# One hybrid decoder layer on one core: the stationary forms of the gate products are made earlier and kept in DRAM, and the order of the product stage changes

## The chip, the cores and the metric

The kernel runs on one core of one Trainium2 chip. The metric is the time of one execution in device microseconds (us). TensorE (PE in the profile) multiplies matrices, VectorE (DVE) and ScalarE (ACT) work on elements, GpSimd (POOL) does small arithmetic and issues transfers, SyncE (SP) issues transfers only. Each engine runs its own instructions strictly in order.

## The reference

One layer on a 256 x 2048 activation x, all in float32:

```python
h = rmsnorm(x, pre_norm_g)
proj = h @ w_in        # split: q_a, c_kv, k_rope, z_mla, c_in, b_gate, c_gate, z_conv, g_mla, g_conv
q, k, v = heads of rmsnorm(q_a) @ w_q_b and rmsnorm(c_kv) @ w_kv_b, with rope
attn = causal_softmax(q, k, v) * silu(z_mla)
y_mla = attn @ w_o_mla
u = c_gate * c_in
conv = sum(conv_w[k] * shifted(u, k) for k in range(3))
y_conv = (b_gate * conv * silu(z_conv)) @ w_o_conv
merged = sigmoid(g_mla) * y_mla + sigmoid(g_conv) * y_conv
out = x + rmsnorm(merged @ w_out, post_norm_g)
```

There are 16 heads; every square weight is 2048 x 2048. All weights are read once from DRAM.

## The kernel before, in words

**Split operands.** A float32 product is made of three reduced-precision products. Each operand is split into `hi` (a rounded copy, made by ACT) and `lo` (the rest, made by DVE as operand minus `hi`); the product is hi·hi + hi·lo + lo·hi. `split_act` does the two instructions. A *unit* is 128 x 2048 numbers (1 MB) of weight: SP loads it into one of three `raw` buffers, ACT and DVE split it in two halves of 1024 columns into `whi` and `wlo` (five buffers each), and PE runs 24 matmuls on it. A weight half in one of the five buffers is free again when PE has used it.

**Stages.** First the two latent projections (`qa`, `ckv`), then a loop over 16 heads. Head h runs four weight units of the convolution branch (`channels`, tile `cv`), at every fourth head four units of `z_mla` (`gates`, tile `z`) and, between them, the small products of the attention. At head 0 the latent vectors are also normalised, turned and split. After the heads comes the product stage, on which most of the change lies: a list `seq` of units, each [load, split, matmuls, after], built by hand.

**The product stage.** It makes, per column block c of 512 columns, the gates (`g_mla` = weight 0, `g_conv` = weight 1 of `wsq`), the branch products with `w_o_mla` (weight 2, left operand `at_both`) and `w_o_conv` (weight 3, left operand `cv_both`), and at the end `w_out` (weight 4, left operand `m_both`).
- A *plain* unit (`plain`, `block`) is the 24 matmuls above, on tile `sq`. `gate_block`, `branch_block`, `merged_block` are blocks of four plain units.
- For c = 1, 2, 3 the two gates are made together by seven products of half size instead of eight (`paired`, Strassen's scheme on 2 x 2 blocks of tokens and features). The left operands are seven *forms*, fixed sums of quarters of the normalised x: `11`, `5`, `6`, `7`, `22`, `3`, `12`. The right operands are sums of weight quarters `b`, made by DVE (128 x 2048 additions): products Q1 and Q2 take a loaded quarter as it is, V5, V6, V4 take a sum, V7 takes a sum of its own, V3 a loaded quarter. Each product is two units of 12 matmuls (tiles `sX`, `sY`, `sZ`); each is split by ACT and DVE like a plain unit (`shi`, `slo`, in the same five buffers).
- `make_forms` makes the seven forms at the start of this stage, from x loaded again (`xf`): 16 scalings, four sums `fs`, seven splits into `form`.
- `interleave` says which plain units stand between the products. The loop at the end of the stage issues loads up to four loads ahead and splits two units ahead.
- `turned_unit` brings a branch's left operand back from DRAM, where it was laid down transposed (`far_at`, `far_cv`, `far_m`), into a `raw` buffer and splits it.
- Gates and partial results that are needed later go to DRAM (`keep`) and come back (`again`), all on POOL's queue. `merged_block` fetches its gate and its partial sum in `last`, after its last matmul; then it multiplies, adds, transposes and stores to `far_m`, from where `m_both` is made for the output projection (`out_order`, `out_product`), which follows at once.

SP's queue holds all weight loads in program order; POOL's holds attention's transfers, the taps, `keep`, `again` and `far_m`. ACT's holds two loads near the end.

## Time and profile before

| | |
|---|---|
| median of 3 runs | 1078.97 us (1078.91 to 1081.7) |
| the profiled execution | 1078.8 us, of which the span is 1076.8 us |
| PE busy | 1024.1 us (95%) |
| DVE busy | 802.2 us (74%) |
| ACT busy | 579.4 us (54%) |
| POOL busy | 196.9 us (18%) |
| moved by DMA | 252.14 MB, mean 234 GB/s |

A busy PE is a PE with a matmul in flight; how fast these run is seen from the granted clock (PEclk, a share of full speed) and from the number of matmuls in a stretch. PE has the largest share, so the time is the sum of its matmuls at full speed and of what it loses by waiting and by a lowered clock.

### The profile page before, as it was taken

The numbers are of one execution on the slowest core, as the hardware profiler recorded it, in microseconds if no ns is written. First come the engines' busy times: TensorE is split into PE (matmuls) and PEld (weight loads), VectorE is DVE, ScalarE is ACT, GpSimd is POOL, SyncE is SP. The second block draws the span as 40 slices with busy tenths as digits, with TensorE's granted clock in tenths as the row PEclk, the third lists the DMA queues.
The fourth block names the chain that finished last, engine by engine and source line by source line (L and its number), as shares of the span: only waits on it lengthen the run. The fifth ranks groups of instructions, "written<-read, shape, count | busy, mean of one in ns | idle before, by whom it ended". The sixth has DMA issues, their size and how long they took to land.

```text
span 1076.8 us, 12835 instructions
## 1 busy us (share of the span) xinstructions
PE 1024.1 (95%) x4576; PEld 846.1 (79%) x4576; DVE 802.2 (74%) x1069; ACT 579.4 (54%) x804; POOL 196.9 (18%) x364
## 2 busy tenths in 40 slices
PE   9999999999999999999999976998999899985997
PEld 7888888888888888888888854886887688873786
DVE  7588777787777877768777799879879887644562
ACT  7666545555455564555645474654565555422451
POOL 4610321223212232122231200000001012223000
PEclk9999999999999999999999998998999899997999
DMA  9775875757657577575867973792586455775752
GB/s 366 284 236 200 284 229 207 251 211 261 231 200 253 211 258 237 194 245 207 273 208 268 339 291 142 260 363 86 192 333 233 155 195 211 234 283 208 260 192 79
DMA packets 49824, 252.14 MB, mean 234 GB/s; under 512 B 8768, under 2 KB 11456, under 8 KB 26592
## 3 DMA queue, kind: packets, MB, share of 16 engines
q1 hardware_dynamic: 33984, 205.96, 53.2%
q0 software_dynamic: 15344, 42.07, 11.7%
q10 hardware_dynamic: 432, 3.29, 0.8%
q8 instruction: 36, 0.59, 0.2%
q14 instruction: 28, 0.23, 0.1%
HBM read 226.15 MB, written 20.97 MB: 229 GB/s over the span
## 4 chain that ended last, share of the span: by engine, by line
PE 85%; DVE 7%; DMA 4%; issue 3%; ACT 1%; POOL 1%; ACTq 0%; DVEq 0%; SPq 0%; POOLq 0%
PE cv L88 32%; PE sq L88 16%; PE z L88 8%; PE out L88 6%; PE sX L88 5%; PE sZ L88 2%; PE kn L88 2%; PE qa L88 2%; PE qn L88 2%; PE vv L88 2%; PE ckv L88 2%; PE sY L88 2%; DVE b L1152 1%; DVE wlo L253 1%; PE qr L88 1%
## 5 line engine op out<-in xcount | busy, mean ns | idle before, releaser
L252 ACT ACTIVATE whi<-raw 128x1024 fp32r<-128x1024 f32 (+1 forms) x318 | 324.2, 1031 | 274.5 <-PE cv L88 126.5
L253 DVE TENSOR_TENSOR wlo<-raw,whi 128x1024 fp32r<-128x1024 f32 (+1 forms) x316 | 371.4, 1190 | 128.2 <-ACT whi L252 119.6
L88 PE MATMUL cv<-whi,x_both 128*128 128x512 f32 x1024 | 319.7, 389 | 0.0
L88 PEld LDWEIGHTS cv<-whi,x_both 128*128 128x128 f32 x1024 | 192.3, 188 | 39.5
L88 PE MATMUL cv<-wlo,x_both 128*128 128x512 f32 x512 | 199.5, 390 | 0.0
L88 PEld LDWEIGHTS cv<-wlo,x_both 128*128 128x128 f32 x512 | 96.2, 188 | 19.4
L252 ACT ACTIVATE shi_V<-b 128x1024 fp32r<-128x1024 f32 x60 | 62.3, 1056 | 75.4 <-DVE b L1152 37.1
L253 DVE TENSOR_TENSOR slo_V<-b,shi_V 128x1024 fp32r<-128x1024 f32 x60 | 72.4, 1222 | 24.7 <-ACT shi_V L252 23.4
L88 PE MATMUL sq<-whi,at_both 128*128 128x512 f32 x256 | 80.8, 389 | 0.0
L88 PE MATMUL z<-whi,x_both 128*128 128x512 f32 x256 | 80.0, 389 | 0.0
L88 PE MATMUL sq<-whi,cv_both 128*128 128x512 f32 x256 | 79.8, 389 | 0.0
L88 PE MATMUL out<-whi,m_both 128*128 128x512 f32 x208 | 67.6, 403 | 7.4 <-ACT whi L252 7.4
L336 POOL DMA_DIRECT2D far<-via x64 | 35.3, 558 | 190.5 <-DVE via L328 189.1
L88 PEld LDWEIGHTS sq<-whi,cv_both 128*128 128x128 f32 x256 | 48.1, 188 | 10.0
L88 PEld LDWEIGHTS sq<-whi,at_both 128*128 128x128 f32 x256 | 48.1, 188 | 9.9
L88 PEld LDWEIGHTS z<-whi,x_both 128*128 128x128 f32 x256 | 48.1, 188 | 9.9
L1152 DVE TENSOR_TENSOR b<-b,b 128x2048 f32<-128x2048 f32 x24 | 54.3, 2284 | 0.6 <-DMA b<-wsq_dram 0.6
L88 PEld LDWEIGHTS out<-whi,m_both 128*128 128x128 f32 x208 | 40.7, 196 | 17.1 <-ACT whi L252 8.6
L88 PE MATMUL sq<-wlo,at_both 128*128 128x512 f32 x128 | 49.9, 390 | 3.3 <-DVE wlo L253 3.3
L88 PE MATMUL out<-wlo,m_both 128*128 128x512 f32 x104 | 42.4, 407 | 10.2 <-DVE wlo L253 10.2
L88 PE MATMUL sq<-wlo,cv_both 128*128 128x512 f32 x128 | 49.8, 389 | 0.0
L88 PE MATMUL z<-wlo,x_both 128*128 128x512 f32 x128 | 49.8, 389 | 0.0
(287 smaller groups left out, 1583.5 us busy)
## 6 DMA issues: line engine op xcount, KB each, us to landing
raw<-wcv_dram SPq DMA_DIRECT2D x64, 1024.0 KB, 5.4
raw<-wsq_dram SPq DMA_DIRECT2D x56, 1024.0 KB, 5.3
b<-wsq_dram SPq DMA_DIRECT2D x24, 1024.0 KB, 5.7
raw<-wz_dram SPq DMA_DIRECT2D x16, 1024.0 KB, 4.8
raw<-wqk_dram SPq DMA_DIRECT2D x8, 1024.0 KB, 6.9
cw<-cwr_dram POOLq DMA_DIRECT2D x24, 256.0 KB, 6.2
raw<-wc_dram SPq DMA_DIRECT2D x4, 1024.0 KB, 9.5
raw<-wv_dram SPq DMA_DIRECT2D x4, 1024.0 KB, 5.3
```

The lines of the kernel that those rows point to most:

```text
L88: return tc.keep_in_program_order(nc.tensor.matmul(*a, **kw))
L252: a = nc.scalar.activation(hi, src, AF.Copy)
L253: b = nc.vector.tensor_tensor(lo, src, hi.bitcast(F32), op=ALU.subtract)
L336: tc.keep_in_program_order(queue.dma_start(out=f[i], in_=m))
L1152: nc.vector.tensor_tensor(t[:, :], t[:, :], raw[plus][:, :], op=ALU.add)
```

## The change

1. **Forms among the heads.** `make_forms` becomes a generator that works on half of the features at a time. During heads 1 to 7 it is stepped three times a head. It loads x into an unused part of `at_f` (four 0.5 MB loads on SP's queue), scales, sums into an unused part of `cv_f`, splits into a small pool, and POOL's queue stores each half form to DRAM (`far_form`, 14 stores of 0.5 MB). At the start of the product stage POOL's queue loads the seven forms (1 MB each) into the place where they were made before.
2. **Order of the product stage.** After each of the seven products of a column block stands, in most places, one plain unit; the second gate block of c = 0 is spread over the products of c = 1.
3. **One sum by DMA.** V7's right operand is no longer added by DVE: after V5 has used quarter `(1, k)`, POOL's queue issues an accumulating load of weight quarter `(1, 2 + k)` onto it. Quarter `(1, 2 + k)` is still loaded for V6.
4. **Gate stores on ACT's queue.** `keep` issues on ACT's queue unless the key is a branch product ("m").
5. **Earlier fetches.** `merged_block` fetches the gate and the partial sum after its second unit (one of the two token halves for c = 0 and 1, both for c = 2 and 3, in a pool `late` of their own). The transposed first two blocks come back a block earlier.

```diff
+    def make_forms():
+
+        kq = KH // 2
+        for c in range(2):
+            area = at_f[:, 8:, :].rearrange("p (i k) s -> p i k s", i=2)
+            for i in range(2):
+                nc.sync.dma_start(out=area[:, i], in_=xf[i][:, c * kq * S : (c + 1) * kq * S].rearrange("p (k s) -> p k s", k=kq))
+            yield
+            for i in range(2):
+                for k in range(kq):
+                    x = area[:, i, k, :]
+                    nc.vector.scalar_tensor_tensor(
+                        x, x, col("pre_g", KH * i + kq * c + k), r_x[:, :], op0=ALU.mult, op1=ALU.mult
+                    )
+                yield
...
+            def part(n, src, sign=1.0):
+                f = early_pool.tile([P, kq, 2, P], F32R, name=f"form{n}_{c}", tag="form", bufs=2)
+                hi, lo = f[:, :, 0, :], f[:, :, 1, :]
+                nc.scalar.activation(hi, src, AF.Copy, scale=sign)
+                if sign == 1.0:
+                    nc.vector.tensor_tensor(lo, src, hi.bitcast(F32), op=ALU.subtract)
...
+                return lambda: tc.keep_in_program_order(
+                    nc.gpsimd.dma_start(
+                        out=far_form[n][:, c * w : (c + 1) * w], in_=f[:, :, :, :].rearrange("p k j c -> p (k j c)")
+                    )
+                )
...
+                if s:
+                    tt(*s)
+                go = part(n, src, sign)
+                yield
+                go()
...
+        if 0 < h < 8:
+            next(form_steps)
         channels(h, 2)
+        if 0 < h < 8:
+            next(form_steps)
+        if 0 < h < 8:
+            next(form_steps)
...
+    for n in FORMS:
+        nc.gpsimd.dma_start(out=form[n][:, :, :, :].rearrange("p k j c -> p (k j c)"), in_=far_form[n][:, :])
...
     def keep(key, t):
-        tc.keep_in_program_order(nc.gpsimd.dma_start(out=kept[key][:, :], in_=t[:, :]))
+        queue = nc.gpsimd if key[0] == "m" else nc.scalar
+        tc.keep_in_program_order(queue.dma_start(out=kept[key][:, :], in_=t[:, :]))
...
     def merged_block(c, both):
...
+        def soon():
+            for t in range(1 if c < 2 else NT):
+                fetch(t)
+
         def last(pss):
             for t in range(NT):
...
+                if len(got) <= t:
+                    fetch(t)
+                g, m = got[t]
...
-        return block(c, 3, lambda k: both[k // 4][:, k % 4, :], {}, last)
+        return block(c, 3, lambda k: both[k // 4][:, k % 4, :], {1: soon}, last)
...
                 t = raw[src]
-                if plus:
+                if plus and name[:2] != "V7":
                     nc.vector.tensor_tensor(t[:, :], t[:, :], raw[plus][:, :], op=ALU.add)
+                if name[:2] == "V5":
+                    k = plus[1]
+                    tc.keep_in_program_order(
+                        nc.gpsimd.dma_start(out=raw[1, k][:, :], in_=wsq[1, c, 2 + k], accum_op=ALU.add)
+                    )
...
-    def interleave(s, p, extra):
-        seq.extend(s["Q1"])
-        seq.extend(extra[:1])
-        seq.extend(s["V5"])
-        seq.extend(extra[1:])
-        for name, n in (("", 1), ("V6", 1), ("V7", 1), ("V4", 2), ("V3", 1), ("Q2", 2)):
-            seq.extend(s.get(name, []))
-            seq.extend(p[:n])
-            del p[:n]
+    def interleave(s, after):
+        for name in ("Q1", "V5", "V6", "V7", "V4", "V3", "Q2"):
+            seq.extend(s[name])
+            seq.extend(after.get(name, []))
...
+    interleave(s1, {
+        "Q1": g0[:1], "V5": g0[1:2], "V6": g0[2:3], "V7": g0[3:] + at_u[:1], "V4": at_u[1:] + p[0][:2],
+        "V3": p[0][2:], "Q2": p[1][:3],
+    })
+    interleave(s2, {
+        "Q1": p[1][3:], "V5": p[2][:1], "V6": p[2][1:2], "V7": p[2][2:3], "V4": p[2][3:], "Q2": p[3][:1],
+    })
+    interleave(s3, {
+        "Q1": p[3][1:2], "V5": p[3][2:3], "V6": p[3][3:] + cv_u[:1], "V7": cv_u[1:] + v[0][:1], "V4": v[0][1:3],
+        "V3": v[0][3:], "Q2": v[1],
+    })
```

How the change moves instructions, at three places. A scheduler places what the program does not pin, so the place of an instruction on its engine is not the place of its line.

**DVE at head 0, where the latent vectors are split and the first weight units of the heads follow** (`wlo` rows are weight splits, `z` the first gate product, `at_f` its area and that of x). Before:

```order
L515 SCALAR_TENSOR_TENSOR ckv<-at_f,pv,ckv 128x256 x4
L740 SCALAR_TENSOR_TENSOR at_f<-z_0_637,r_both,at_f 128x512
L328 STREAM_TRANSPOSE cw<-at_f 128x4x4x32
L740 SCALAR_TENSOR_TENSOR at_f<-z_1_638,r_both,at_f 128x512
L253 TENSOR_TENSOR wlo_0_812<-raw_761,whi_0_811 128x512
L253 TENSOR_TENSOR wlo_0_816<-raw_807,whi_0_815 128x1024
L328 STREAM_TRANSPOSE cw<-at_f 128x4x4x32
L253 TENSOR_TENSOR wlo_1024_820<-raw_807,whi_1024_819 128x1024
```

After:

```order
L517 SCALAR_TENSOR_TENSOR ckv<-at_f,pv,ckv 128x256 x4
L840 SCALAR_TENSOR_TENSOR at_f<-at_f,pv,r_x 128x256 x4
L742 SCALAR_TENSOR_TENSOR at_f<-z_0_647,r_both,at_f 128x512
L851 TENSOR_TENSOR cv_f<-at_f 128x512 x2
L330 STREAM_TRANSPOSE cw<-at_f 128x4x4x32
L858 TENSOR_TENSOR form_0_1588<-at_f,form_0_1588 128x4x128
L851 TENSOR_TENSOR cv_f<-cv_f,at_f 128x512
L858 TENSOR_TENSOR form_0_1622<-at_f,form_0_1622 128x4x128
L742 SCALAR_TENSOR_TENSOR at_f<-z_1_648,r_both,at_f 128x512
L253 TENSOR_TENSOR wlo_0_822<-raw_771,whi_0_821 128x512
L253 TENSOR_TENSOR wlo_0_826<-raw_817,whi_0_825 128x1024
L253 TENSOR_TENSOR wlo_1024_830<-raw_817,whi_1024_829 128x1024
```

Work on the forms (L840, L851, L858) that the text puts into heads 1 to 3 stands here, at head 0; one more sum (L851) and four more scalings (L840) of the next half stand within the eight rows after the last one shown, still ahead of the splits of the second unit of head 0. Four scalings stand still earlier, before the `z` splits.

**SP and POOL at the end of the heads, where the product stage's loads begin** (`raw` are plain units, `b_n_k` weight quarters of c = 1, `xf` is x). SP before:

```order
L164 DMA raw_5692<-wsq_dram 128x2048
L981 DMA xf_5588<-xf_dram 128x2048
L981 DMA xf_5590<-xf_dram 128x2048
L164 DMA raw_5731<-wsq_dram 128x2048
L1144 DMA b_0_0_5779<-wsq_dram 128x2048
L1144 DMA b_0_1_5822<-wsq_dram 128x2048
L1064 DMA turned_0_5856<-far_at_624 128x1024
```

SP after:

```order
L164 DMA raw_5958<-wsq_dram 128x2048
L1174 DMA b_0_0_5694<-wsq_dram 128x2048
L1174 DMA b_0_1_5738<-wsq_dram 128x2048
L1174 DMA b_1_0_5806<-wsq_dram 128x2048
L1174 DMA b_1_1_5848<-wsq_dram 128x2048
L1174 DMA b_1_2_5897<-wsq_dram 128x2048
L1174 DMA b_1_3_5935<-wsq_dram 128x2048
L164 DMA raw_5981<-wsq_dram 128x2048
```

POOL after, following the last stores of the heads:

```order
L1033 DMA form_5672<-far_form_640 128x2048
L1033 DMA form_5673<-far_form_641 128x2048
L1033 DMA form_5674<-far_form_642 128x2048
L1033 DMA form_5675<-far_form_643 128x2048
L1033 DMA form_5676<-far_form_644 128x2048
L1033 DMA form_5677<-far_form_645 128x2048
L1033 DMA form_5678<-far_form_646 128x2048
L1186 DMA b_1_0_5806<-wsq_dram 128x2048
L1186 DMA b_1_1_5848<-wsq_dram 128x2048
```

Where SP held two loads of x and two of `b`, it holds six loads of `b` in a row, and POOL holds seven form loads and behind them the first two accumulating loads (L1186).

**DVE at the second paired block, c = 2, around V5** (`slo_Q` is a split of Q1, `slo_V` of V5 and V6; the rows that write `b` are the weight sums). Before:

```order
L1152 TENSOR_TENSOR b_0_0_6350<-b_0_0_6350,b_1_0_6509 128x2048
L1152 TENSOR_TENSOR b_1_0_6509<-b_1_0_6509,b_1_2_6611 128x2048
L253 TENSOR_TENSOR slo_Q_1_6550<-b_0_1_6430,shi_Q_1_6549 128x1024
L1110 TENSOR_TENSOR y_0_6577<-sq_0_6360,y_0_6577 128x512
L1110 TENSOR_TENSOR y_1_6579<-sq_1_6361,y_1_6579 128x512
L253 TENSOR_TENSOR slo_V_0_6591<-b_0_0_6350,shi_V_0_6590 128x1024
L253 TENSOR_TENSOR slo_V_1_6595<-b_0_0_6350,shi_V_1_6594 128x1024
L1152 TENSOR_TENSOR b_0_1_6430<-b_0_1_6430,b_1_1_6543 128x2048
L1152 TENSOR_TENSOR b_0_0_6350<-b_0_0_6350,b_1_2_6611 128x2048
L1152 TENSOR_TENSOR b_1_1_6543<-b_1_1_6543,b_1_3_6636 128x2048
L253 TENSOR_TENSOR slo_V_0_6615<-b_0_1_6430,shi_V_0_6614 128x1024
```

After:

```order
L253 TENSOR_TENSOR slo_Q_0_6574<-b_0_1_6501,shi_Q_0_6573 128x1024
L1182 TENSOR_TENSOR b_0_0_6412<-b_0_0_6412,b_1_0_6571 128x2048
L253 TENSOR_TENSOR slo_Q_1_6578<-b_0_1_6501,shi_Q_1_6577 128x1024
L253 TENSOR_TENSOR wlo_0_6608<-raw_6537,whi_0_6607 128x1024
L1182 TENSOR_TENSOR b_0_1_6501<-b_0_1_6501,b_1_1_6605 128x2048
L253 TENSOR_TENSOR wlo_1024_6612<-raw_6537,whi_1024_6611 128x1024
L253 TENSOR_TENSOR slo_V_0_6633<-b_0_0_6412,shi_V_0_6632 128x1024
L253 TENSOR_TENSOR slo_V_1_6637<-b_0_0_6412,shi_V_1_6636 128x1024
L253 TENSOR_TENSOR slo_V_0_6659<-b_0_1_6501,shi_V_0_6658 128x1024
L1182 TENSOR_TENSOR b_0_0_6412<-b_0_0_6412,b_1_2_6654 128x2048
```

Two sums of V7 are gone from the row of sums, and the remaining ones stand singly between splits, of which two belong to a plain unit (`wlo`).

129 lines of the change are left out of this document (57 added, 72 removed).

## Prediction

> **What bounds the kernel now.** I read the engine totals first, then what PE waits for, then the stages.
>
> ```profile
> PE 1024.1 (95%) x4576; PEld 846.1 (79%) x4576; DVE 802.2 (74%) x1069; ACT 579.4 (54%) x804; POOL 196.9 (18%) x364
> PEclk9999999999999999999999998998999899997999
> ...
> PE sZ L88 <- DVE slo_V L253: 16.6, 4, 7.7
> PE out L88 <- DVE wlo L253: 10.2, 4, 5.7
> PE out L88 <- ACT whi L252: 7.4, 3, 4.2
> PE sZ L88 <- ACT shi_V L252: 7.0, 3, 3.7
> PE sq L88 <- DVE wlo L253: 3.3, 1, 3.3
> PE sX L88 <- DVE slo_Q L253: 1.5, 1, 1.5
> ```
>
> PE is the bound and waits 46 us in all (the six rows of waits), only in the product stage (sX, sZ, sq) and in the output projection (out); the clock dips in the same slices. The stretches, with their matmul counts and granted clock, say where:
>
> ```profile
> 589.50:668.00 78.50, 62.19 (x261) 49.65 (x260) 71.34 (x77) 40.54 (x48) 7.17 (x13) 0.91 0.71 262
> 668.00:742.00 74.00, 74.00 (x328) 61.31 (x327) 58.72 (x50) 42.55 (x44) 6.54 (x12) 1.00 0.70 262
> 742.00:757.00 15.00, 9.77 (x34) 7.32 (x34) 14.93 (x11) 6.96 (x7) 0.00 (x0) 0.77 0.18 70
> 830.00:846.00 16.00, 9.08 (x27) 6.30 (x26) 16.00 (x12) 6.87 (x8) 2.17 (x4) 0.68 0.46 160
> 959.00:1010.00 51.00, 33.41 (x125) 25.51 (x125) 22.07 (x25) 15.05 (x18) 11.05 (x20) 0.87 0.66 236
> ...
> 589.50 9.57 PE sq L88 x42
> ...
> 758.48 5.44 PE sX L88 x24
> ```
>
> After the times stand PE, PEld, DVE, ACT, POOL busy with their counts, the clock, the DMA share and GB/s. In the chain of waits the product stage begins at 589.5, and 24 matmuls take 5.44 us at full clock, 0.227 us each. So the first stretch needs 261 x 0.227 = 59.2 of its 78.5 us and loses **19.3**; the second loses nothing; then 34 matmuls (7.7 us) in 15: **7.3**; 27 (6.1) in 16: **9.9**; 125 (28.3) in 51: **22.7**. Together 59.2 us: 46 of waits, 13 of lowered clock around them. With none of it this execution of 1078.8 us would take 1019.6. In the first three losing stretches DVE is busy for 71 of 78, 14.9 of 15 and 16 of 16 us: DVE is what PE waits for. In the last it is busy 22 of 51.
>
> **The change part by part.** *The paired blocks.* Prices on DVE:
>
> ```profile
> L253 DVE TENSOR_TENSOR slo_V<-b,shi_V 128x1024 fp32r<-128x1024 f32 x60 | 72.4, 1222 | 24.7 <-ACT shi_V L252 23.4
> L1152 DVE TENSOR_TENSOR b<-b,b 128x2048 f32<-128x2048 f32 x24 | 54.3, 2284 | 0.6 <-DMA b<-wsq_dram 0.6
> L990 DVE SCALAR_TENSOR_TENSOR xf<-xf,pv,r_x 128x256 f32<-128x256 f32 x16 | 6.5, 479 | 2.8 <-DMA xf<-xf_dram 2.8
> L253 DVE TENSOR_TENSOR wlo<-raw,whi 128x512 fp32r<-128x512 f32 x18 | 12.3, 684 | 0.0
> ```
>
> A unit's split costs DVE 2 x 1.22 = 2.44 us. PE needs 5.44 us for a plain unit, 2.72 for one of a product. A product with a sum (V5, V6, V4) costs DVE 2 x (2.28 + 2.44) = 9.4 us against 5.44 on PE; with a plain unit behind it, 11.9 against 10.9; V7 without its sum and with a plain unit, 7.3 against 10.9. Before, V5 of c = 2 and 3 follows Q1 directly: 4.9 + 9.4 = 14.3 us of DVE against 10.9, and the sums of V6 and V7 stand ahead of its splits. That is the loss at 742 and 830. Per block of seven products DVE has 14 x 2.44 + 6 x 2.28 + 5 results x 0.68 = 51 us. For c = 2 with its six plain units that is 66 against PE's 14 x 2.72 + 6 x 5.44 = 70.7; for c = 1 with eight plain units and 8 x 0.68 for `at_both`, 76 against 81.6; for c = 3 with seven, as much for `cv_both` and 6 x 0.68 of merging, 78 against 76.2. DVE fits, barely, and not at c = 3. I leave 1.5 us of loss at c = 2 (of 7.3; bounds 0 and 7.3, the loss before) and 3.5 at c = 3 (of 9.9; bounds 1.5, about the tally's excess, and 9.9). The two add up to a gain of 5.8 + 6.4.
>
> *The start of the stage.* The forms' 16 scalings (6.5 us) and 11 instructions of 1.22 leave DVE here, about 20 us, which covers the old cause of the 19.3. What is late next is data. At 602 us the loads come free (the row of the xf load below), and Q1 now starts after one gate block instead of two: 589.5 + 4 x 5.44 = 611.
>
> ```profile
> 600.00:610.00 10.00, 10.00 (x45) 8.26 (x44) 4.90 (x4) 4.10 (x5) 1.91 (x4) 1.00 0.98 355
> 610.00:620.00 10.00, 10.00 (x46) 8.27 (x45) 8.96 (x19) 6.12 (x7) 0.73 (x2) 1.00 1.00 409
> ...
> 601.89 9.13 DMA xf<-xf_dram
> ...
> b<-wsq_dram SPq DMA_DIRECT2D x24, 1024.0 KB, 5.7
> ```
>
> The transfers are already full there (share 0.98 and 1.00), at 409 GB/s. In the place of xf stands the first b load; behind it five more and a plain unit, and beside them seven forms from POOL: 14 loads of 1.05 MB, 14.7 MB, 36 us at 409 GB/s. If SP's loads get half of it, one takes 5.1 us: the first b is there at about 613, the second at 618. A half is split 2.3 us later, so Q1 starts 4 us late, its second unit waits 3 more, V5's second 1.5. I take 9 us of this, 2 for what DVE leaves: 11 of the 19.3 stay, a gain of 8.3. Bounds: 2 (no wait for data) and 25 (all 14 loads and the two accumulating ones come before PE goes on).
>
> The Trainium skill bears on it: "DMA: Bandwidth & Descriptors", section "Issuing engines are not separate DMA queues", says that transfers from all issuing engines run on the same 16 DMA engines and interleave. It speaks against loading the forms on POOL's queue as a way around SP's. By it the 9 us stand; if POOL's queue had room of its own, the term would be 0. The share of 1.00 agrees with the page, but no row before shows the two queues both full.
>
> *The accumulating load.* No row shows one. Below, it costs a b load (5.7 us); above, nothing in the trace bounds it. It has time: issued when V5 has been added, needed when V7 is split, with V5, a plain unit, V6 and a plain unit between, 4 x 5.44 = 21.8 us, for two loads. I take twice the plain load, 11.4 us each, partly overlapped, hidden: 0 us.
> The skill's "Collectives: The Full Stack", section "The bandwidth ceiling: the fold count and why AG ≠ RS ≠ AR", says that an add in the DMA path costs a second source read and that the ALU adds nothing. An estimate from it is also twice a copy; no run here shows it.
>
> *The forms among the heads.* Heads 1 to 7 have PE at 100% with DVE at 75%:
>
> ```profile
> 300.00:400.00 100.00, 100.00 (x464) 83.69 (x463) 75.47 (x118) 56.25 (x84) 22.41 (x41) 1.00 0.66 229
> ```
>
> The forms in halves are 16 x 0.41 + 22 x 0.68 = 21.5 us on DVE, spread over two hundred: 0 on PE; the free quarter of DVE hides them, as it does the 9 MB of transfers at a DMA share of 0.66. But the order above shows that part of it stands at head 0, and there DVE has no room:
>
> ```profile
> 75.97 0.75 DVE L740 SCALAR_TENSOR_TENSOR at_f<-z,r_both,at_f 128x512 f32<-128x512 f32 x1 [1.91 <-ACT at_f L739]
> 91.53 5.24 DVE L253 TENSOR_TENSOR wlo<-raw,whi 128x1024 fp32r<-128x1024 f32 x5 [0.28 <-ACT whi L252]
> ...
> 93.14 0.40 PE L88 MATMUL cv<-wlo,x_both 128*128 128x512 f32 x1
> ```
>
> The first of these five splits ends at 92.75 and PE uses it at 93.14: 0.4 us to spare. Ahead of it come 8 scalings and 6 instructions of 0.68, 3.3 + 4.1 = 7.4 us; idle time such as the 1.91 takes up about 2.5. So PE loses about **5 us**, a new loss (bounds 0, if more idle time takes them, and 9, with a lowered clock behind it).
>
> *The end.* What PE waits for in the last 51 us is a circle through three queues:
>
> ```profile
> DVE vg L1128 <- DMA vg<-kept_gc: 26.8, 4, 10.4
> ...
> 971.80 0.57 POOL L1064 DMA_DIRECT2D turned<-far_m  x1 [9.66 <-DMA raw<-wsq_dram]
> ...
> SPq L164 <- DMA turned<-far_m: 25.1, 3, 11.6
> ...
> vg<-kept_gc POOLq DMA_DIRECT2D x8, 256.0 KB, 4.8
> far_m<-vg POOLq DMA_DIRECT2D x32, 64.0 KB, 2.5
> turned<-far_m POOLq DMA_DIRECT2D x4, 512.0 KB, 4.2
> ```
>
> DVE waits for gates fetched after the last matmul, so `far_m` is late, so the turned load holds a `raw` buffer, and SP's weight loads wait for it. With the fetches early, 0.7 us steps remain: from the end of a block about 7 us on DVE, 4.4 for eight issues on POOL, 2.5 and 4.2 to land: 18 us, then the split. For column block 2 the 21.8 us of block 3 cover it. For block 3 it runs beside three to four output units (16 to 22 us); the fifth and sixth unit's splits and one weight load stand behind it. I leave 5 of the 22.7 us (bounds 2 and 14): a gain of 17.7. The gate stores on ACT's queue wait only for ACT's own results: 0, ACT is busy 54%.
>
> **Sum.** 8.3 + 5.8 + 6.4 + 17.7 - 5 = 33.2; 1078.8 - 33.2 = **1045.6 us**, which I give as 1046. The profiled execution lies 0.2 us under the median shown, so nothing is corrected.
>
> **Rivals.**
> - *Nothing new waits*: the data are in time at the start (2 us stay), head 0 absorbs its work, 0, 1.5 and 2 us stay later. Gain 17.3 + 7.3 + 8.4 + 20.7 = 53.7: **1025 us**. For it: 74 us of PE without a wait from 668. Against: the DMA share of 1.00, and 0.4 us to spare.
> - *DVE stays the bound at c = 2 and 3*, any bubble being kept because 66 of 70.7 and 78 of 76.2 leave nothing to catch up with: 12.2 us less gain, **1058 us**. Against: from 668 to 742 DVE needs 58.7 of 74.
> - *The end keeps its circle*, since turned loads still share the `raw` buffers: 17.7 less, **1063 us**. Against: DVE's 26.8 us on the fetch.
> - *Slower: the accumulating load is slow.* V7 waits at each of three blocks. The gain is gone when each waits 11 us, that is when a pair takes over 33 us. At four times a plain load and one after the other, 45.6 us, V7 waits 23.8 three times, 71 us: **1117 us**. For it: no row; against: nothing but its 22 us of room.
> - *It does not do what it says*: only if the scheduler undid the order, which the rows above exclude.
>
> **Chances.** Forecast 0.63, nothing new waits 0.12, DVE 0.13, the end 0.06, accumulation 0.05, no effect 0.01. The range of the likeliest is 1034 to 1057. For 8 in 10, from just under the first rival to just over the third: **1023 to 1066**. This kernel can tell about 0.3%, 3 us, from no change. Faster 0.93, same 0.02, slower 0.05.
>
> **What would show it.** In the profile after: waits of sZ for slo_V under 5 us in all; Q1 (sX) waiting for ACT's shi_Q or DVE's slo_Q behind DMA b, with a DMA share near 1 from 602 to 640; a wait at cv near 93 us; out waiting under 6 us, and no DVE wait on kept_gc over 3. Wrong, if sX or sZ waits at V7 behind the accumulating load, if the first 580 us lose over 9, or if the DMA share after 602 stays under 0.8 while PE waits.

## The result, and the profile after

Twelve executions of each kernel: 1074.98 us after (1070.06 to 1077.95), 1080.12 us before (1078.42 to 1083.33). The ratio is **0.9949 [0.9932, 0.9965]**: faster by 0.5%, some 5 us. The prediction was 1046 us, a gain of 33. The sign is right; five sixths of the gain are missing. The profiled execution took 1075.9 us with a span of 1074.1.

First the engine totals and the DMA totals of the page after.

```profile
PE 1032.0 (96%) x4576; PEld 850.0 (79%) x4576; DVE 786.3 (73%) x1074; ACT 577.5 (54%) x811; POOL 205.4 (19%) x373
...
DMA packets 55152, 273.12 MB, mean 254 GB/s; under 512 B 9232, under 2 KB 11920, under 8 KB 30512
```

DVE lost 16 us of work, as the change intends, and 21 MB more are moved. The rest is in PE's waits and in the stretches in which they fall. The first fence has what PE waits for (total us, times, longest); the second has the windows, in the columns of the prediction.

```profile
PE sX L88 <- ACT shi_Q L252: 6.3, 1, 6.3
PE out L88 <- ACT whi L252: 6.2, 2, 3.7
PE out L88 <- DVE wlo L253: 4.0, 3, 2.7
PE kn L88 <- DVE at_f L742: 3.6, 2, 3.1
PE sc L88 <- DVE kn L253: 3.5, 1, 3.5
PE sX L88 <- DVE slo_V L253: 3.5, 2, 2.2
PE sq L88 <- DVE wlo L253: 2.6, 2, 2.2
PE sZ L88 <- DVE slo_V L253: 2.1, 2, 1.3
```

```profile
626.00:658.00 32.00, 22.32 (x75) 16.64 (x75) 20.05 (x15) 15.00 (x16) 2.92 (x4) 0.79 1.05 412
658.00:684.00 26.00, 26.00 (x116) 21.49 (x116) 20.50 (x17) 13.09 (x14) 0.00 (x0) 1.00 0.97 322
684.00:704.00 20.00, 14.94 (x57) 11.34 (x56) 17.50 (x19) 15.46 (x22) 0.00 (x0) 0.91 0.77 298
704.00:826.00 122.00, 122.00 (x540) 101.02 (x539) 99.75 (x84) 73.20 (x75) 6.91 (x12) 1.00 0.74 259
826.00:850.00 24.00, 22.26 (x97) 17.77 (x96) 22.40 (x21) 15.38 (x20) 2.15 (x3) 1.00 0.83 233
...
958.00:1008.00 50.00, 39.84 (x145) 30.83 (x144) 22.04 (x25) 15.18 (x17) 8.76 (x16) 0.86 0.76 289
```

With 0.227 us a matmul, as in the prediction, the stretch from 626 needs 75 x 0.227 = 17.0 of 32 us and loses 15.0; that from 684 loses 7.1; the 122 us from 704, in which c = 2 lies, lose nothing; that from 826 (c = 3) loses 2.0; the last loses 17.1. The wait of sZ for slo_V, the largest of before with 16.6 us, is 2.1. What was removed is gone; other waits stand in its place.

Both kernels run the same 4576 matmuls, and those of one stage come in the same number, so the start of the k-th matmul in the two traces tells where the time went (k counted from 0):

| matmul, place | before | after | after minus before |
|---|---|---|---|
| 300th, first gate product of head 0 | 69.56 | 70.66 | +1.1 |
| 400th, head 0 | 90.17 | 98.22 | +8.05 |
| 1230th, head 4 | 267.98 | 276.93 | +8.95 |
| 1300th, head 4 | 283.26 | 297.87 | +14.6 |
| 2400th, before the product stage | 520.54 | 535.36 | +14.8 |
| 3060th, behind V4 of c = 1 in after | 686.30 | 704.00 | +17.7 |
| 3360th, in V6 of c = 2 | 761.95 | 772.00 | +10.1 |
| 3900th, behind c = 3 | 894.57 | 897.20 | +2.6 |
| 4260th, output projection | 995.74 | 987.53 | -8.2 |
| 4575th, the last one | 1071.75 | 1068.83 | -2.9 |

So the heads lose 14.8 us, the first paired block 2.9 more; c = 2 gains 7.7, c = 3 gains 7.4, the end 5.5. The rows at 3060 and 3360 stand inside a column block; from either of them to the end of its block the difference stays the same.

**Head 0.** DVE's timeline there (start, busy, instruction, idle time before it and what ended it), and PE's:

```profile
76.30 1.67 DVE L840 SCALAR_TENSOR_TENSOR at_f<-at_f,pv,r_x 128x256 f32<-128x256 f32 x4 [2.29 <-DMA at_f<-xf_dram]
77.89 0.74 DVE L742 SCALAR_TENSOR_TENSOR at_f<-z,r_both,at_f 128x512 f32<-128x512 f32 x1
78.55 1.28 DVE L851 TENSOR_TENSOR cv_f<-at_f 128x512 f32<-128x512 f32 x2
...
82.15 0.74 DVE L742 SCALAR_TENSOR_TENSOR at_f<-z,r_both,at_f 128x512 f32<-128x512 f32 x1
```

```profile
82.94 2.07 PE L88 MATMUL kn<-ckv,whi 128*128 128x512 f32 x4 [3.06 <-DVE at_f L742]
```

The form scalings (L840) do not only take time: DVE stands 2.3 us at them for the load of x, with the gates (L742) that PE needs behind them, and the form sums stand between the two gates. PE waits 0.6 + 3.1 us, and its clock is 0.5 for 6.8 us behind that, which costs about 3.

**Head 4.** ACT's timeline, then PE's:

```profile
276.03 0.63 ACT L856 ACTIVATE form<-at_f 128x512 fp32r<-128x512 f32 x1 [9.11 <-DMA far_form<-form]
276.57 2.94 ACT L252 ACTIVATE whi<-raw 128x1024 fp32r<-128x1024 f32 x3
```

```profile
286.58 0.39 PE L88 MATMUL sc<-kn,qn_hi 128*128 128x256 f32 x1 [3.51 <-DVE kn L253]
```

The half forms have two buffers. ACT stands 9.1 us at a form until the store of the form two before it has landed (issued at 267.6, there at 276.0), and three weight splits stand behind it. Ten us later PE waits for the attention's operands.

**The start of the product stage.** Loads, from the timelines of SP and POOL, and PE's first product:

```profile
616.71 5.93 SPq L1174 DMA_DIRECT2D b<-wsq_dram  x6
```

```profile
616.30 1.12 POOL L1033 DMA_DIRECT2D form<-far_form  x2
```

```profile
632.38 0.80 PE L88 MATMUL sX<-shi_Q,form 128*128 128x512 f32 x1 [6.26 <-ACT shi_Q L252]
```

Six quarters and seven forms are issued within 6 us. Their landings alternate: form 626.8, b 631.3, form 632.3, b 636.5, form 637.4, b 642.0. Up to 658 PE waits 6.26 + 0.46 + 2.23 + 0.74 = 9.7 us, and a clock of 0.5 around the waits takes the other 5 of the 15.0. (The plain unit that stands on SP's queue ahead of the quarters lands first, at 625.9.)

**The end.** The chain of waits, and ACT's timeline:

```profile
977.93 4.86 DMA far_m<-vg
...
983.50 11.58 DMA turned<-far_m
```

```profile
967.70 1.99 ACT L252 ACTIVATE whi<-raw 128x1024 fp32r<-128x1024 f32 x2
983.08 0.34 ACTq L1399 DMA_DIRECT2D gb<-post_g_dram  x1
983.45 0.46 ACTq L1400 DMA_DIRECT2D xr<-x_dram  x1
984.03 2.00 ACT L252 ACTIVATE whi<-raw 128x1024 fp32r<-128x1024 f32 x2 [14.34 <-issue]
995.11 1.15 ACT L252 ACTIVATE m_both<-turned 128x512 fp32r<-128x512 f32 x2 [9.07 <-DMA turned<-far_m]
```

`gb` and `xr` are the two loads that ACT issues for the last normalisation (3 MB). Their space is now that of the new pool `late`, so the issue on ACT waits until the last `far_m` store has landed, at 982.8; in before the same issue went out at 959.2. ACT stands 13.4 us, the output's weight splits behind it; then 3 MB run beside the last turned load, which takes 11.6 us where the other three take 3.7 to 5.9. Of the 17.1 us that this stretch loses, 10.2 are waits of `out` and the rest clock.

### The profile page after: what moved, and what is told of

Its sections match the earlier page's. It is cut to its first block, busy times and chain, and to the rows that moved or that the text cites. A ratio compares the mean times of both kernels' runs of the same rounds, so it can differ in the third digit from the quotient of the medians.

```text
span 1074.1 us, 12900 instructions
## 1 busy us (share of the span) xinstructions
PE 1032.0 (96%) x4576; PEld 850.0 (79%) x4576; DVE 786.3 (73%) x1074; ACT 577.5 (54%) x811; POOL 205.4 (19%) x373
## 3 DMA queue, kind: packets, MB, share of 16 engines
q1 hardware_dynamic: 34272, 205.96, 53.7%
q0 software_dynamic: 17792, 58.32, 17.2%
## 5 line engine op out<-in xcount | busy, mean ns | idle before, releaser
L88 PEld LDWEIGHTS z<-whi,x_both 128*128 128x128 f32 x256 | 48.1, 188 | 11.1 <-DVE at_f L406 1.2
L253 DVE TENSOR_TENSOR slo_Q<-b,shi_Q 128x1024 fp32r<-128x1024 f32 x24 | 29.2, 1224 | 28.6 <-ACT shi_Q L252 27.3
L88 PE MATMUL sX<-shi_V,form 128*128 128x512 f32 x144 | 47.0, 397 | 1.6 <-ACT shi_V L252 1.6
```

Of the source, the lines that this page charges most:

```text
L88: return tc.keep_in_program_order(nc.tensor.matmul(*a, **kw))
L253: b = nc.vector.tensor_tensor(lo, src, hi.bitcast(F32), op=ALU.subtract)
```

## The experiments

Each kernel is compared with before, as after was; "against after" is the difference of the two ratios times 1079.5 us. Where an edit moves one stage, the start of the k-th matmul says more than the whole time, since single times of after alone spread over 8 us.

The theory after the result: four separate places, each an in-order queue with something late at its head, hold back the gain. The rivals are named in the expectations.

**Heads: the order of the form work.** `e1_heads` pins the form instructions where the text has them and moves the steps to heads 2, 3, 6 and 7, which have no gate products:

```diff
-        if 0 < h < 8:
+        if h in (2, 3, 6, 7):
+            next(form_steps)
             next(form_steps)
         channels(h, 2)
...
-                    nc.vector.scalar_tensor_tensor(
+                    tc.keep_in_program_order(nc.vector.scalar_tensor_tensor(
```

> The forms' vector and scalar instructions are held to their program order, and their steps stand in heads 2, 3, 6 and 7 only, so that none runs in heads 0 and 4, where DVE also has the gates of a group to finish. Theory: the 14.8 us that PE lost over the heads (7.9 of it in head 0 up to 89 us, 5.7 at 283 us in head 4) come from DVE's queue being in order, form work standing ahead of at_f and kn; then the time lost up to 600 us falls to 0 to 3 us, the waits kn<-at_f (3.6) and sc<-kn (3.5) are gone, and the time is 1060 to 1064 (0.982 to 0.985 of before). Rival: the loss comes from the traffic of the forms' loads and stores (11 MB more among the heads); then the loss stays near 15 us and the time near 1075 (0.995).

Measured: 0.9907 [0.9887, 0.9928], 1069.06 us, 4.5 us against after. The waits of kn and sc are gone, and by the 1320th matmul 13.8 of the 14.8 us are back; 3.9 are lost again at 303, where ACT stands 4.4 us at a form for a store, as at head 4. So the form work at heads 0 and 4 is the cause of most of the heads' loss; whether its order or its place is, this run, which changes both, does not tell. But 6 of the 10 us won are given back in c = 1, where another order of ACT's queue lets PE wait 5.9 us for V4:

```profile
676.99 2.19 ACT L252 ACTIVATE at_both<-turned 128x512 fp32r<-128x512 f32 x4 [3.45 <-PE sq L88]
...
681.74 1.99 ACT L252 ACTIVATE shi_V<-b 128x1024 fp32r<-128x1024 f32 x2
```

The splits of the turned operand `at_both`, which nobody needs yet, stand ahead of V4's first split. In after shi_V came first.

`e5_bufs` is e1_heads with one form buffer more:

```diff
-                f = early_pool.tile([P, kq, 2, P], F32R, name=f"form{n}_{c}", tag="form", bufs=2)
+                f = early_pool.tile([P, kq, 2, P], F32R, name=f"form{n}_{c}", tag="form", bufs=3)
```

> The form work held in heads 2, 3, 6 and 7 as in the first run of the heads, and three buffers for a form's half on its way to DRAM instead of two. Theory: of the 4.9 us that the heads still lost there, 3.9 came at 303 us, where a form's ACT instruction waited 4.4 us for the store of the form two before it, and ACT's queue, cv_w in it, waited behind; with a third buffer the heads lose under 2 us, and the time is 1064 to 1067 (3 to 5 below the run with two buffers), or 1067 to 1069 if the stage behind, which gave back 4 of the 10 us won there, swallows this too. Rival: the stores are late because the transfers are full; a third buffer only moves the wait, heads lose 4 to 5 us as before, 1069.

Measured: 0.9879 [0.9862, 0.9895], 1066.3 us, 7.6 against after. ACT's waits for form stores, of after, of e1_heads and of e5_bufs:

```profile
ACT form L856 <- DMA far_form<-form: 16.4, 7, 9.1
```

```profile
ACT form L856 <- DMA far_form<-form: 14.8, 5, 4.4
```

```profile
ACT form L856 <- DMA far_form<-form: 5.9, 2, 4.0
```

The heads now lose 1.7 us where after lost 14.8. What the third buffer adds to e1_heads is not shown, though: at 301 ACT still stands 3.95 us at a form for a store where it stood 4.4, the intervals of the two kernels overlap, and e12_last below, with three buffers as well, loses 4.3 us at this place, more than the 3.9 of e1_heads. The rival, that a third buffer only moves the wait, is not excluded.

**Start: the order and the amount of the loads.** `e2_loads` puts each form load on SP's queue ahead of the quarter it belongs to; `e6_few` loads three forms instead of seven. It leaves the other four forms out, and their products use one of the three, so it stands for time alone.

```diff
-    for n in FORMS:
-        nc.gpsimd.dma_start(out=form[n]...
+    need = {(0, 0): ("11",), (1, 0): ("5",), (1, 2): ("6",), (1, 3): ("7",), (0, 2): ("22",), (0, 3): ("3", "12")}
+    def form_loads(c, n, k):
+        for f in need.get((n, k), ()) if c == 1 else ():
+            nc.sync.dma_start(out=form[f]...
...
                 raw[n, k] = t
+                form_loads(c, n, k)
```

> The seven form loads go on SP's queue, each right behind the weight load of the product that uses it, instead of all at once on POOL's queue beside the weight loads. Same bytes, another order. Theory (order): at 616.5 us 13 loads of 1 MB start together on two queues and share 411 GB/s, so the first weight block that Q1 needs lands 14.5 us later; in the order of use the first block and the first form land in 2 x 2.6 us, by 622, before Q1 at 626. The wait sX<-shi_Q (6.3) goes, with the half clock behind it (10.2 us, 5.1 lost), the 2.2 at 643 and its half clock: 12 to 16 us, time 1059 to 1063 (0.981 to 0.984). Rival (volume): 13.6 MB from 616 on are too much in any order; Q1's wait goes but comes back at V5 and at the plain units, gain under 5 us, 1070 to 1075.

```diff
-    form = {n: forms.tile([P, KH, 2, P], F32R, name=f"form_{n}") for n in FORMS}
-    for n in FORMS:
+    form = {n: forms.tile([P, KH, 2, P], F32R, name=f"form_{n}") for n in FORMS[:3]}
+    form.update(zip(FORMS[3:], [form[n] for n in FORMS[:3]] * 2))
+    for n in FORMS[:3]:
```

> Only three of the seven forms are loaded and the other four products use one of these three (that part of the computation is wrong): 4.2 MB less at the start of the stage, all else as changed. Theory (volume): from 616 to 680 us the transfers run at a share of 1.0, so the loads themselves bound the stage, and in an order of use (second run) only 2 us could be won; 4.2 MB less at 411 GB/s are 10 us: Q1's wait of 6.3 and the waits up to 656 us with their half clock (14 us) fall to a third, while the 5 us at V4 (685 to 691, transfer share 0.42, DVE 0.98) stay; time 1063 to 1068. Rival (the stage is bound by DVE and by the lead of the splits, transfers only hide it): under 3 us, 1072 to 1075.

Measured: e2_loads 0.9930 [0.9902, 0.9957], 1072.68 us, 2.1 against after, within what can be told. In its profile Q1's first wait falls from 6.3 to 3.0 us and c = 1 gains 3.2. e6_few 0.9865 [0.9844, 0.9887], 1065.59 us, 9.1 against after, of which c = 1 shows 7.1 in the profile; the rest lies in the heads, which the edit does not touch. Its window from 626 to 658 (its heads are 2.9 us shorter than those of after, so it has come further there):

```profile
626.00:658.00 32.00, 27.68 (x107) 21.62 (x108) 27.44 (x21) 18.43 (x20) 2.92 (x4) 0.90 1.03 347
```

107 matmuls where after had 75; with the window moved 2.9 us ahead, 96. So the start is short of transfer time: 4.2 MB less give 7 us, a better order of all of them 3. The edit also lets the two accumulating loads start 2.2 and 4.6 us earlier in the stage; how much of the 7 us that is, was not separated. Transfers are full here in either case (shares 1.05 and 1.03).

**End: who issues gb and xr.**

```diff
-    nc.scalar.dma_start(out=gb[:, :], in_=post_g.to_broadcast([P, D]))
-    nc.scalar.dma_start(out=xr[:, :, :], in_=x)
+    nc.gpsimd.dma_start(out=gb[:, :], in_=post_g.to_broadcast([P, D]))
+    nc.gpsimd.dma_start(out=xr[:, :, :], in_=x)
```

> The loads of gb and xr (3 MB, needed only at the very end) are issued by POOL behind the last turned load, instead of by ACT. Theory: their buffers reuse the space of the early fetched gates, so ACT's queue stood 14.3 us (969.7 to 984.0) at gb's wait for the far_m stores, with the output units' splits behind it, and the 3 MB then ran beside the last turned load, which took 11.6 us instead of 5. With the edit the waits of out for ACT at 982.7 (2.4 + 0.8) and at 993.5 (3.8 + 0.5) go, with some 5 us of half clock behind them: gain 8 to 12 us, time 1063 to 1067 (0.985 to 0.988). Rival (the circle of the prediction): the turned load waits for far_m behind DVE's and POOL's steps, and the weight loads for the buffer that it holds; then under 3 us are gained, 1072 to 1075.

Measured: 0.9857 [0.9826, 0.9887], 1065.21 us, **9.9 against after with two lines changed**. Its ACT timeline and its waits:

```profile
986.60 1.16 ACT L252 ACTIVATE m_both<-turned 128x512 fp32r<-128x512 f32 x2 [3.38 <-DMA turned<-far_m]
```

```profile
PE out L88 <- DVE wlo L253: 4.2, 2, 3.4
PE out L88 <- ACT whi L252: 1.8, 1, 1.8
```

The last turned load lands 3.7 us after its issue instead of 11.6, ACT no longer stands, and `out` waits 6.0 us where it waited 10.2. The theory holds; the rival, that the circle through the `raw` buffers still sets the end, fell. ACT's stand and the slow turned load went together, so the run does not say what each was worth.

`e7_fetch` adds to it that block 3's fetches are issued with those of block 2, ahead of the turned load on POOL:

```diff
+            if c == 2:
+                fetch_last[0]()
...
-        return block(c, 3, lambda k: both[k // 4][:, k % 4, :], {1: soon}, last)
+        if c == 3:
+            fetch_last.append(soon)
+        return block(c, 3, lambda k: both[k // 4][:, k % 4, :], {} if c == 3 else {1: soon}, last)
```

> As the run with gb and xr on POOL, and the six fetches for merged column block 3 are issued with those of block 2, so that they do not stand in POOL's queue behind the turned load of block 2, which waits for its far_m stores (6.2 us). Theory: DVE waits for the late vg and vq (2.0 + 0.6 us) with the split of the first output units behind it; the wait of out for wlo at 971 (3.4 us, with 3.4 us of half clock) falls under 1: 3 to 5 us under the run with gb on POOL, 1060 to 1062. Rival: DVE's own merging (eight instructions, 6.5 us) is what stands ahead of that split; then no gain, 1064 to 1066.

Measured: 0.9847 [0.9811, 0.9883], 1063.01 us: no difference from e3_gb, and `out` still waits 3.1 us for wlo. The rival was right: in its profile DVE's last waits ahead of that split are for PE (1.7 and 0.6 us), not for a fetch, and its merging then stands ahead of the split up to 966.4.

**The accumulating load.** `e4_noacc` gives V7's sum back to DVE:

```diff
-                if plus and name[:2] != "V7":
+                if plus:
                     nc.vector.tensor_tensor(t[:, :], t[:, :], raw[plus][:, :], op=ALU.add)
-                if name[:2] == "V5":
-                    k = plus[1]
-                    tc.keep_in_program_order(
-                        nc.gpsimd.dma_start(out=raw[1, k][:, :], in_=wsq[1, c, 2 + k], accum_op=ALU.add)
-                    )
```

> The accumulating load is undone: V7's sum is made on DVE again, all else as changed. The prediction's view: the accumulating load costs PE nothing, while the sum costs DVE 4.6 us per block, which takes c = 2 from 66 to 71 of 70.7 us and c = 3 from 78 to 83 against 76; so 2 to 8 us slower than the changed kernel, 1077 to 1083 (0.997 to 1.003). Rival: the accumulating loads (12.4 us to landing against 5.9 of a plain one, 6 MB more traffic) are what keeps c = 1 slow; then 2 to 5 us faster, 1070 to 1073 (0.990 to 0.993).

Measured: 1.0046 [1.0021, 1.007], 1084.7 us, **slower by 10.5** than after and slower than before. That is more than the 2 to 8 us expected. By the k-th matmul 5.1 lie in c = 1, for which nothing had been expected, 2.1 in c = 2, 3.7 in c = 3. Its wait row that answers to the 2.1 us of after, and its DMA queues beside those of after:

```profile
PE sZ L88 <- DVE slo_V L253: 8.6, 4, 3.4
```

```profile
q1 hardware_dynamic: 34272, 205.96, 53.2%
q0 software_dynamic: 16928, 52.03, 14.4%
```

```profile
q1 hardware_dynamic: 34272, 205.96, 53.7%
q0 software_dynamic: 17792, 58.32, 17.2%
```

Without the accumulating load c = 2 still gains 5.5 of its 7.7 us over before, and c = 3 3.7 of its 7.4: most of the gain at c = 2 and half of it at c = 3 come without this edit (by the tally of DVE, from the plain units between the products), the rest comes from it. Its price in transfer time: 17.2% of 1074.1 less 14.4% of 1080.0, 29.2 us for 6.29 MB, is 4.6 us of all engines per MB, against 2.8 (53.7% of 1074.1 for 205.96 MB) of the plain transfers of the other queue.

**The gate stores.** `e10_gates` is after with all `keep` stores on POOL:

```diff
-        queue = nc.gpsimd if key[0] == "m" else nc.scalar
+        queue = nc.gpsimd
```

> The changed kernel with its gates stored by POOL's queue again, all else as changed. The prediction's view: the queue of the gate stores is worth nothing, within 2 us of the changed kernel, 1073 to 1077 (0.993 to 0.997). Rival: POOL's queue, in which the accumulating loads and the fetches now stand as well, holds them up behind a gate that is not ready; then V7 waits for its sum or the merging for its fetches, 3 to 8 us slower, 1078 to 1083.

Measured: 0.9914 [0.9883, 0.9944], 1069.42 us, under both ranges: the rival, slower, is excluded. The intervals of this kernel and of after overlap. The profile shows 10 us less, but 5.7 of them at head 4, which the edit does not touch: ACT's form there waited 3.7 us for its store, not 9.1. So nothing can be said of the queue itself.

The seven profiles of kernels whose heads have the text of after (after, e2_loads, e3_gb, e4_noacc, e6_few, e7_fetch and this one) show head 4 more clearly than any edit. ACT's wait at that form is 3.0 (e4_noacc), 3.7, 8.2, 9.1, 9.2, 9.9 and 10.1 us (e3_gb), and the time that PE loses there is 0, 0, 4.8, 5.7, 5.7, 7.7 and 6.6. By the 2700th matmul the same head text loses between 7.5 and 18.0 us, with the forms pinned in e1_heads and the runs built on it between 0.8 and 4.8. What makes this store land in 4 us or in 8 to 9 was not settled.

**All together.** `e8_all` joins e5_bufs, e2_loads and e7_fetch.

> All edits in one: form work in heads 2, 3, 6 and 7 with three buffers, forms loaded on SP's queue in the order of use, gb and xr on POOL, fetches for block 3 with those of block 2. If the four losses are separate, the gains add up: 8 in the heads, 2 at the start, 10 at the end, 3 by the fetch, about 1052 to 1056 (0.976 to 0.979). If the volume of loads sets the start of the stage, what the heads win is given back there, and the time is 1058 to 1062 (0.981 to 0.984).

Measured: 0.9733 [0.9711, 0.9754], 1049.42 us, 23.3 against after. Taken alone the three gave 7.6 + 2.1 + 11.0 = 20.7: within the intervals, the losses are separate and add up. The largest of what is left is V4 of c = 1:

```profile
PE sX L88 <- ACT shi_V L252: 5.9, 1, 5.9
...
PE sX L88 <- DVE slo_V L253: 3.8, 3, 3.2
```

`e9_swap` therefore lets V3, which needs no sum, come before V4 in c = 1 and puts the two units of `at_both` behind V3 and behind V4 (the last argument names the order of the two products):

```diff
-    interleave(s1, {
-        "Q1": g0[:1], "V5": g0[1:2], "V6": g0[2:3], "V7": g0[3:] + at_u[:1], "V4": at_u[1:] + p[0][:2],
-        "V3": p[0][2:], "Q2": p[1][:3],
-    })
+    interleave(s1, {
+        "Q1": g0[:1], "V5": g0[1:2], "V6": g0[2:3], "V7": g0[3:], "V3": at_u[:1],
+        "V4": at_u[1:] + p[0], "Q2": p[1][:3],
+    }, ("V3", "V4"))
```

> On top of the run with all edits: in column block 1 alone product V3 comes ahead of V4, and the units of at_both stand behind V3 and V4 instead of ahead of and behind V4's first place. What it tells apart: in that run V4 waited 5.9 and 3.2 us at 666 to 673, with 10.2 us of half clock behind (14 us in all). Theory: V4's second weight block can only be loaded when V7's split has let its buffer go (it landed at 665), and ACT and DVE work on at_both, which waits for the last plain unit with x_both, ahead of V4's split; V3 needs no load, so V4 gets 5.4 us more; V4's wait falls under 3 us and 8 to 12 us are won: 1038 to 1042 (0.962 to 0.966). Rival (the transfers are full until 680 in any order): the wait comes back at V4 or at the plain units, under 4 us won, 1046 to 1049.

Measured: 0.9697 [0.9659, 0.9735], **1045.28 us, 3.0% under before and the fastest of all**, though its interval overlaps e8_all's. By the k-th matmul c = 1 wins 2.6 us of the expected 8 to 12: ACT's wait is gone, DVE's is not.

```profile
PE sX L88 <- DVE slo_V L253: 6.1, 3, 4.1
...
PE sX L88 <- DMA form<-far_form: 2.6, 1, 2.6
```

```profile
672.15 3.10 DVE L253 TENSOR_TENSOR at_both<-turned,at_both 128x512 fp32r<-128x512 f32 x5
...
675.76 4.63 DVE L253 TENSOR_TENSOR slo_V<-b,shi_V 128x1024 fp32r<-128x1024 f32 x4
```

In DVE's queue the splits of `at_both` still stand ahead of V4's, after V4's last sum has ended at 672.2 and with ACT's part of V4's first split done by 672.4; PE's 4.1 us wait ends at 677.0. An order that puts both units of `at_both` behind V4 was not tried.

Two attempts to go on from e9_swap failed. `e11_lead` puts one more plain unit ahead of Q1, to give the loads time:

```diff
+    seq.extend(g0[:1])
     interleave(s1, {
-        "Q1": g0[:1], "V5": g0[1:2], "V6": g0[2:3], "V7": g0[3:], "V3": at_u[:1],
+        "Q1": g0[1:2], "V5": g0[2:3], "V6": g0[3:], "V3": at_u[:1],
```

> On top of the run that puts V3 ahead of V4: one plain unit more ahead of Q1 (the first of the gate block that is spread through column block 1), none behind V7. Same work, same bytes; Q1 starts 5.4 us of PE later, and its loads have so much more time from 616 us on. Theory: the 13 loads that come free together are a backlog that only time or fewer bytes take away; Q1's wait (2.6) and the ones behind it to 646 us (1.2, 0.8, 0.5, 1.6, with 3.4 us of half clock) go, 5 to 7 us; V4, which now has one plain unit less ahead of it, waits up to 3 us more: 1039 to 1044. Rival: these waits come from the lead of the splits, and V4's wait grows by the whole unit: 1045 to 1050.

Measured: 0.9781 [0.9758, 0.9805], 1055.19 us, about 10 slower than e9_swap: theory and rival both missed. Q1's second unit waits 8.8 us, though its quarter had landed at 617.6. ACT's timeline:

```profile
613.93 0.67 ACT L1108 ACTIVATE sg<-sq,r_both 128x512 f32<-128x512 f32 x1
627.45 0.33 ACTq L1027 DMA_DIRECT2D kept_gm<-sg  x1
627.88 2.00 ACT L252 ACTIVATE shi_Q<-b 128x1024 fp32r<-128x1024 f32 x2 [13.28 <-DMA b<-wsq_dram]
```

A gate store on ACT's queue, whose data are ready at 614.6, is issued at 627.45, just after another quarter load of SP has landed (627.38). In this program the transfers of SP and of ACT share eight completion semaphores in turn, and this store's turn came on the one that the late load still held (the trace names number 105 for both). Q1's split stood behind it. The second new loss is a wait of 5.0 us of V3 for DVE, which still adds the result in the same PSUM tile, behind splits of V4 and `at_both`.

`e12_last` takes the gate stores off ACT in e9_swap, by the edit of e10_gates.

> The run with V3 ahead of V4 (all edits, 1045.3 us), and the gates stored by POOL's queue again. With the forms on SP's queue the store of a gate stood on ACT's queue for 3.0 us (12.9 in the run with one more plain unit) with the split of Q1's second block behind it. Theory: that wait goes with the queue; Q1's waits for ACT and for its second unit (1.2, 0.8 and 3.4 us of half clock) go, 2 to 5 us: 1040 to 1043 (0.964 to 0.967). Rival: on POOL the stores stand in front of the accumulating loads and the fetches, and hold these; then no gain, 1045 to 1049.

Measured: 0.9737 [0.9711, 0.9762], 1050.54 us, no gain over e9_swap's 1045.28. The theory fell: in e9_swap the store at which ACT stands for 3.0 us goes out at 618.4, and the quarter that the split behind it needs lands at 618.5; here, with no store in the way, the split waits for the same quarter until 621.3. So those 3.0 us cost nothing.

## Why the prediction was right or wrong

**Right, with their sizes.** c = 2: 5.8 predicted, 7.7 measured, and nothing of its loss stays; c = 3: 6.4 against 7.4, with 2.0 left of 3.5. The wait of sZ for slo_V under 5 us: 2.1. The load waits at the start: 9 us predicted, 9.7 measured, of which the sum fits better than its parts (6.3 where 4 was computed, 0.5 for 3, 2.2 for 1.5), with a quarter landing every 5.2 us where 5.1 was computed from half of 409 GB/s. The Trainium skill ("DMA: Bandwidth & Descriptors", section "Issuing engines are not separate DMA queues") had the two queues interleave on the same engines, and the alternating landings agree. The accumulating load: 11.4 us each predicted, 9 to 14 in c = 2 and 3, about 20 in c = 1 where transfers are full, hidden every time, so the term of 0 was right. e4_noacc adds what no sum had: the edit is worth 5.1 us in c = 1 too.

**Heads: the term of 5 was 14.8.** Two steps failed. First, only the duration of the added DVE work was counted (7.4 us less idle time). The instruction at its head waits for a load of its own, 2.3 us, with everything behind it, and a lowered clock follows; the wait comes at kn near 83 us, not at cv near 93. The bound of 9 us for head 0 had held the clock, and head 0 with 8.05 lies within it. Second, "the forms in halves ... 0 on PE" for heads 1 to 7: that counted how busy DVE and the DMA engines are, and not that ACT, in order, would stand at a form for a buffer whose store is on its way. A quarter of free DVE time hides no wait in ACT's queue. e1_heads shows that the form work there is what costs the time, 14.8 becoming 4.8, and the seven profiles with the same head text show the store: no loss at head 4 where ACT waits 3 to 4 us, 5 to 8 us where it waits 8 to 10.

**Start: the 11 us kept were 22.1.** The mechanism was right and its price incomplete. The 9 us counted the wait for data without the clock behind it, 5 us, although the tally of before had 13 us of clock beside 46 of waits. And it followed the loads only as far as V5. Transfers stay full to 684 (share 0.97), and 7.1 us are lost at V4, from 684 to 704, where DVE splits at_both between V4's halves. The tally of DVE by column block (76 against 81.6) gave no room for such an order inside the block. e6_few puts 7 us on the loads; e9_swap won 2.6 of V4's share, and in its profile `at_both` still stands on DVE ahead of V4's splits.

**End: the 5 us kept were 17.1.** The step that failed is the sentence that costs ACT's queue by its 54% of busy time. It looked at the gate stores, and not at the two loads already on that queue, whose space the new pool moved to a later release. The circle was broken as computed (DVE's wait on kept_gc is 4.5 us, down from 26.8), but the limit went to ACT. e3_gb shows the size: about 10 us. The 18 us computed from the end of block 3 to the landing of its turned load were 33 (961.7 to 995.1): the turned load took 11.6 for 4.2, the last `far_m` store 4.9 for 2.5, and DVE's steps 12 for 7, with vq, which POOL issued only at 966.2 behind the turned load of block 2, landing at 971.2.

**The rivals.** "Nothing new waits" is excluded by four new waits; "DVE stays the bound at c = 2 and 3" by the 122 us without a loss and the 2.0 us left at c = 3; "the accumulating load is slow" by landings with no wait at V7, and e4_noacc shows that this edit is worth 10 us. "The end keeps its circle" was nearest in size, but through another queue.

**The prediction's own signs.** Of those named for being right, sZ for slo_V (2.1 us), Q1's wait for shi_Q behind the quarters at a full DMA share (0.95 to 1.04 from 616.5 to 640) and kept_gc (2.0 at most) came; the wait at cv near 93 and `out` under 6 us (it waited 10.2) did not. One of those for being wrong came: the first 580 us lost 14.8, over 9.

The three terms that missed by 10 to 12 us each (9.8 + 11.1 + 12.1 = 33) add up to more than what is missing of the gain, since c = 2 and 3 gave more than predicted. Heads and end have one form: the wait of an in-order queue was costed by its engine's busy share. The start's term lacked the clock behind its waits and a second late place, V4. With most of this repaired, e9_swap runs at 1045.28 us, beside the 1046 that the prediction had given for the change as it stood. That agreement is partly chance: V4's loss at the start is still there, and c = 2 and 3 gained more than predicted.

## What to carry to other kernels

Work moved into "free" engine time must be costed by what the first instruction of it waits for and by who stands behind it in that queue; buffers with a store in flight and transfers issued from a computing engine are the usual places. A new pool can change which release a later tile waits for, so look up who takes over its space, and give such late loads to an engine that nobody waits for. When a removed bound was 46 us of waits, look for the next thing late in each stage separately: here each repair kept its worth beside the others.

## What the runs showed of the hardware

**The clock falls after shorter waits than expected.** After the 2.45 us wait of `out` at 982.7 the windows of after show:

```profile
985.00:986.80 1.80, 0.90 (x3) 0.55 (x4) 1.68 (x2) 1.04 (x2) 0.00 (x0) 1.00 1.00 423
986.80:990.20 3.40, 3.40 (x10) 2.66 (x9) 0.68 (x1) 0.00 (x0) 0.00 (x0) 0.50 1.03 428
990.20:993.40 3.20, 3.20 (x15) 2.39 (x13) 0.00 (x0) 0.00 (x0) 0.00 (x0) 1.00 1.01 431
```

Exactly 0.5 for 3.4 us, in which PE is busy throughout but starts 8 matmuls where 15 would fit (10 reach into the window). All such stretches lasted 3.4, 6.8 or 10.2 us (13.7 once, before), but for the last of each execution, which its end cuts off. The Trainium skill ("TensorE: Matmul & The Clock Gate", section "HAM oscillation — how this bites in real kernels") gives an idle gap of over about 3.4 us as the condition; the half rate and the length of the steps agree with this case, the condition does not.

The length of a wait alone does not decide it: 1.91 us at 304.9 of e1_heads had a stretch behind it; 2.12 us at 961.2 of before, 2.23 at 640.7 of e4_noacc and 2.27 at 639.9 of e6_few had none. In each of the fourteen profiles all these stretches begin and end on one grid of 3.413 us (to within 0.002), whose place differs from run to run. Cut along this grid, PE's idle time tells the cases apart. Of the pieces at full clock, all with more than 1.82 us of idle time had half clock behind them and none with less than 1.77; the half clock began 74 times, and some 4000 pieces had none behind them. So a wait of about 2 us brings the half clock if it falls into one piece, and does not if the grid cuts it in two. Where it does, it costs itself and some 1.6 us more for each step of 3.4 us (the 7 matmuls of 0.227 us that are missing above).

**An accumulating load** took 1.7 times the transfer time of a plain one (an estimate from the queues' shares: 4.6 against 2.8 us per MB), where the prediction had taken twice.

**An issue on ACT's queue can stand for 13 us** with all of ACT's arithmetic behind it: for its space (gb, 13.4 us) or for a completion semaphore still held by another engine's load (12.9 us in e11_lead). The store of a half form, 0.5 MB, took 3.8 to 9.4 us at the same place in different kernels with the same code there; why was not found.
